# The scale of four RMS norms: a power of 256 columns on every partition in place of a power of two columns and a diagonal

## Chip, cores and metric

The kernel runs on one core of a Trainium2 chip. The metric is the device time of one execution in microseconds; the figure for the kernel before is the median of three runs. The traces come from one profiled execution. TensorE is called PE here (PEld is its weight load), VectorE DVE, ScalarE ACT, GpSimd POOL and SyncE SP; SP issues the transfers.

## What is computed

One step of a two-layer backbone for 128 context tokens and 128 latent tokens. Each layer has a mixer (layer 0: latent attention beside grouped-query attention; layer 1: differential attention) and a gated FFN with a width-3 convolution. Ahead of each mixer and each FFN, and once at the end, stands an RMS norm over the 2048 features of a token:

```python
def rmsnorm(x, g):
    xf = x.astype(jnp.float32)
    y = xf * lax.rsqrt(jnp.mean(xf * xf, axis=-1, keepdims=True) + EPS)
    return (y * g.astype(jnp.float32)).astype(x.dtype)
...
for l in range(DEPTH):
    mod = jax.nn.silu(cond) @ w_ada[l] + b_ada[l]
    sh1, sc1, gt1, sh2, sc2, gt2 = jnp.split(mod[:, None, :], 6, axis=-1)
    h = rmsnorm(x, g_norm_mix[l]) * (1 + sc1) + sh1
    m, new = mixer(h)
    x = x + gt1 * m
    h = rmsnorm(x, g_norm_ffn[l]) * (1 + sc2) + sh2
    x = x + gt2 * conv_ffn(h, ...)
return rmsnorm(x, g_final)
```

All weights are float32, and the adaLN product `silu(cond) @ w_ada` (two rows of condition against 2048 x 12288 per layer) is spread through the program, a piece at a time, beside the large products.

## The kernel before

**Layout.** Features lie on the 128 partitions and tokens on the free axis: `x` is a tile of 128 x 16 x 256, that is 16 chunks of 128 features, with the 128 context and 128 latent tokens side by side in 256 columns. The mean of squares of a token is therefore a sum over partitions, for which TensorE is used, and its scale is wanted on all partitions, since every chunk is multiplied by it column by column.

**Products.** Each float32 weight block is split into a high and a low half of type float32r (`split`: ACT makes `wh` by a cast, DVE makes `wl` by a subtraction), and the activations `hx` likewise. A block of 128x128 then takes three products of 256 columns (L299 to L301 for the first three output chunks after a norm, in `first_three`; L313, L314 and L317 elsewhere, in `gemm`).

**The norm's sums.** While the last product of a stage runs, `residual` adds each finished chunk to `x` (L569), ACT squares it into `sq` (L171), and POOL adds it to a running sum `sqacc` (L175). The square of the last chunk isn't added; it enters the sum as a second product.

**The scale before.** `stat_rstd` multiplies `sqacc` and `sq`, as the stationary operand, by a column of 1/2048: four products with one output column (L200, L201), which leave the mean of squares of each token on a partition, one column for the context tokens and one for the latent ones. `rstd` adds EPS on DVE (L183, 128x2) and takes the power -0.5 on POOL (L187, 128x2). `diagonal` multiplies the identity by each of the two columns (L207, two DVE instructions of 128x128), and `spread` multiplies `ones` by the result (L215, 128x256): the scale of each token stands on all partitions, in PSUM. This is done at four places after the opening: by `modulated` before the FFN of layer 0, before the mixer of layer 1 and before the FFN of layer 1, and by `norm_scale` at the end. The same helpers serve norms inside the mixers. The norm that opens layer 0 has sums of its own and is not touched.

**What follows the scale.** `modulate` makes `hx` chunk by chunk: DVE multiplies `x` by the scale (L510), DVE and ACT apply scale and shift (L516, L519), ACT casts to the high half (L520), and POOL or DVE subtracts for the low half (L505). `first_three` begins with the first chunks that are ready. At the end of the program, 16 DVE instructions (L1104) scale `x` into the result, and SP stores four chunks at a time.

**Order.** A scheduler with a timeline of its own orders the instructions of each engine; instructions under `keep_in_program_order` stay as written. In the two places of layer 1, `modulate` and `first_three` are so fixed; before the FFN of layer 0 they are not. `modulated` also carries a piece of the adaLN product: the tiles `araw` of `w_ada` (two buffers, four tiles of 1 MB a unit) are loaded by SP, `sum_rows` multiplies each (L427, four products of 512 columns), ACT copies the sum, and four PE transposes (L376) turn it. Some adaLN pieces run on DVE instead (`feature_sum`, L404).

Of the kernel before, what the change touches and what calls it, by code (L numbers as in the profile page):

```python
# [14 lines left out]
ALU = mybir.AluOpType  # L15
# [3 lines left out]
P = 128  # L19
D = 2048  # L20
KD = D // P
T = 128
NT = 2 * T
# [4 lines left out]
EPS = 1e-6  # L28
# [56 lines left out]
def step_kernel(ctx: ExitStack, tc: tile.TileContext, A: dict):  # L85
    nc = tc.nc
    pe, dve, act, pool, sp = nc.tensor, nc.vector, nc.scalar, nc.gpsimd, nc.sync
# [3 lines left out]
    tmp = ctx.enter_context(tc.tile_pool(name="tmp", bufs=2))  # L91
# [12 lines left out]
    def nm(s):  # L104
        uid[0] += 1
        return f"{s}_{uid[0]}"

    def T_(pl, shape, tag, dt=F32, bufs=None):
        kw = {} if bufs is None else {"bufs": bufs}
        return pl.tile(shape, dt, tag=tag, name=nm(tag), **kw)  # L110
# [8 lines left out]
    def C(name):  # L119
        a, w = _AT[name]  # L120
        return cst[:, a:a + w]

    ident, ones = C("ident"), C("ones")

    def inv(n):
        a = _AT["inv"][0] + INV[n]
        return cst[:, a:a + 1]
# [32 lines left out]
    def stat_init():  # L160
        return {"acc": None, "n": 0, "last": None}
# [15 lines left out]
    def rstd(cols, n, factor=1.0, out=None):  # L177

        v = T_(small, [P, 2], "rv")
        at = 0  # L180
        for ps in cols:
            w = n // len(cols)
            dve.tensor_scalar(out=v[:, at:at + w], in0=ps, scalar1=EPS, scalar2=factor ** -2,  # L183
                              op0=ALU.add, op1=ALU.mult)
            at += w
        r = T_(small, [P, 2], "rr") if out is None else out
        pool.tensor_tensor(out=r[:, :n], in0=v[:, :n], in1=C("mhalf")[:, :n], op=ALU.pow)  # L187
        return r

    def bank():  # L190
        return T_(pmisc, [P, 512], "misc")

    def att_bank():
        return T_(ppool["att"], [P, 512], "att", bufs=3)

    def stat_rstd(st, width, bank=bank, **kw):
        ps = bank()
        for g in range(2):
            t = slice(g * T, (g + 1) * T)
            pe.matmul(ps[:, g:g + 1], st["acc"][:, t], inv(width), start=True, stop=False)  # L200
            pe.matmul(ps[:, g:g + 1], st["last"][:, t], inv(width), start=False, stop=True)  # L201
        return rstd([ps[:, 0:2]], 2, **kw)

    def diagonal(r, cols):
        dg = T_(tmp, [P, 2 * T], "diag", bufs=1)
        for i, c in enumerate(cols):
            dve.tensor_scalar(out=dg[:, i * T:(i + 1) * T], in0=ident, scalar1=r[:, c:c + 1],  # L207
                              scalar2=None, op0=ALU.mult)
        return dg

    def spread(dg, cols=(0, 1), bank=bank):

        ps = bank()
        n = len(cols) * T
        pe.matmul(ps[:, :n], ones, dg[:, :n], start=True, stop=True)  # L215
        return ps[:, :n]
# [146 lines left out]
    def ada_finish(l, j, q):  # L363

        got = dict(ada)

        def copy():
            am = T_(tmp, [P, 512], "am", bufs=1)
            act.copy(am, got["ps"])
            got["am"] = am  # L370

        def turn(pin=None):
            pt = bank() if pin else T_(ppool["ada"], [P, 512], "ada", bufs=1)
            pin = pin or (lambda i: i)
            for b in range(4):
                pin(pe.transpose(pt[:, b * P:(b + 1) * P], got["am"][:, b * P:(b + 1) * P], ident))  # L376
            out = mod[:, l, j, 4 * q:4 * q + 4]
            dve.tensor_reduce(out=out, in_=pt.rearrange("p (b g r) -> p b r g", b=4, g=4)[:, :, 0:2],
                              axis=AX.X, op=ALU.add)
            biased(l, j, q)  # L380

        return [copy, turn]
# [40 lines left out]
    def sum_rows(t, raw, ps=None):  # L423
        if t == 0:
            ada["ps"] = ps or T_(ppool["ada"], [P, 512], "ada", bufs=1)
        for g in range(4):
            i = pe.matmul(ada["ps"][32 * g:32 * g + 32, :], condw[:, 4 * t + g, :], raw[:, g],  # L427
                          start=(t == 0), stop=(t == 3), skip_group_check=True)
            if pinned[0]:
                tc.keep_in_program_order(i)  # L430
# [53 lines left out]
    def ensure(l, j, qs=range(4)):  # L484
        for u in [(l, j, q) for q in qs]:
            while u in ROWS and ada["i"] <= ROWS.index(u):
                row_step()
            while u in FEATS and u not in done:
                feature_step()
            while u not in done:  # L490
                later.pop(0)()


    def norm_scale(st):
        return spread(diagonal(stat_rstd(st, D), (0, 1)))

    def modulate(hx, rb, l, which, chunks, fixed=False):


        pin = tc.keep_in_program_order if fixed else lambda i: i  # L500
        lows = []

        def low(c, h):
            eng = dve if (c % 4 == 0 if fixed else c % 2 == 0) else pool
            pin(eng.tensor_tensor(out=hx[:, c, NT:2 * NT], in0=h, in1=hx[:, c, :NT].bitcast(F32),  # L505
                                  op=ALU.subtract))

        for c in chunks:
            h = T_(tmp, [P, NT], "nt", bufs=4)
            pin(dve.tensor_tensor(out=h, in0=x[:, c], in1=rb, op=ALU.mult))  # L510
            for g in range(2):
                s = slice(g * T, (g + 1) * T)
                a_ = scl[:, l, which, c, g:g + 1]
                b_ = mod[:, l, 3 * which, c, g:g + 1]
                if g == 0:
                    pin(dve.tensor_scalar(out=h[:, s], in0=h[:, s], scalar1=a_, scalar2=b_,  # L516
                                          op0=ALU.mult, op1=ALU.add))
                else:
                    pin(act.activation(h[:, s], h[:, s], AF.Identity, scale=a_, bias=b_))  # L519
            pin(act.copy(hx[:, c, :NT], h))  # L520
            lows.append((c, h))
            if not fixed or len(lows) > 1:
                low(*lows.pop(0))
        for c, h in lows:
            low(c, h)

    def modulated(st, l, which, W, fixed):


        ensure(l, 3 * which + 1)  # L530
        ensure(l, 3 * which)
        while later:
            later.pop(0)()
        u = ROWS[ada["i"]]
        tile_ = lambda t: T_(wpool, [P, 4, 512], "araw", bufs=2)

        def load_tile(t):
            raw = tile_(t)
            sp.dma_start(out=raw, in_=A["w_ada"][u[0], u[1], u[2], t])
            return raw  # L540

        raws = [load_tile(0), load_tile(1)]
        hx = T_(keep, [P, KD, ROW], "hx", F32R)
        r = stat_rstd(st, D, att_bank)
        sum_rows(0, raws[0], bank())
        rb = spread(diagonal(r, (0, 1)), bank=att_bank)
        sum_rows(1, raws[1])
        raws += [load_tile(2), load_tile(3)]
        modulate(hx, rb, l, which, range(KD), fixed)
        ada["i"] += 1  # L550
        rest = ada_finish(*u)

        def last_rows():
            sum_rows(3, raws[3])
            rest[0]()

        def turn():
            rest[1](tc.keep_in_program_order)

        ps = first_three(W, lambda k: hx[:, k, :NT], lambda k: hx[:, k, NT:2 * NT],  # L560
                         AS_MADE if fixed else IN_TURN, lambda: sum_rows(2, raws[2]), fixed)
        if fixed:
            W.ahead(lambda i: i)
        return hx, ps, [last_rows, turn]
# [500 lines left out]
    with banks("pab") as ppool["ada"]:  # L1065
# [4 lines left out]
        ps = [bank(), att_bank()]  # L1070
# [9 lines left out]
        st = stat_init()  # L1080
# [4 lines left out]
    st = stat_init()  # L1085
    ffn(hx, W, ready, todo, 0, st)
    stage[0] = "c"
    with tc.tile_pool(name="cc", bufs=1) as cp, banks("pc") as ppool["ada"]:
        ada["pool"] = cp
        ppool["att"] = ppool["ada"]  # L1090
        W = Weights(A["w_in_c"], KD, 1)
        hx, ready, todo = modulated(st, 1, 0, W, True)
        load_cw(1)
        st = stat_init()
        ada["pew"] = PEW["c"]
        mixer_c(cp, hx, W, ready, todo, st)
        W = Weights(A["w_up"][1], KD, 1)
        hx, ready, todo = modulated(st, 1, 1, W, True)
    stage[0] = "ffn1"
    st = stat_init()  # L1100
    ffn(hx, W, ready, todo, 1, st)
    rb = norm_scale(st)
    for c in range(KD):
        dve.scalar_tensor_tensor(out=x[:, c], in0=x[:, c], scalar=C("gfin")[:, c:c + 1], in1=rb,  # L1104
                                 op0=ALU.mult, op1=ALU.mult)
# [132 lines left out]
```

## Time and profile before

| | us |
|---|---|
| median of 3 runs | 2371.13 (2369.91 to 2372.9) |
| profiled execution, its own time | 2370.48 |
| span of its trace (first to last instruction) | 2368.7 |
| TensorE busy | 2308.6 (97%) |
| DVE busy | 1798.8 (76%) |
| ACT busy | 1173.3 (50%) |
| POOL busy | 136.0 (6%) |

The mean granted clock of TensorE is 0.989 of full speed, and the DMA queues moved 610.81 MB. In a timeline each row gives the start, the time from the first start to the last end of the instructions merged in it, the engine, the line, the operation, the output and inputs by their names in the program, and in brackets how long the engine had been idle and what ended that. A row of the window table gives the busy time of each engine in a stretch of the span, with the count of its instructions, and at the end the granted clock, the share of DMA time and the rate. A row of a tile gives least, median and greatest duration in ns, and the first and last start.

### The profile page before, as it was taken

The page shows a single profiled execution, that of the slowest core. Times are in us where ns is not written, and L with a number is a line of the kernel's source. Part 1 is how long each engine was busy: PE and PEld are TensorE (multiplying, and loading weights), DVE is VectorE, ACT ScalarE, POOL GpSimd, SP SyncE. Part 2 cuts the span into 40 slices and gives each one's busy share as a digit, 9 for nine tenths or more (in the row PEclk, how much of TensorE's full clock was granted, in tenths as well). Part 3 has the DMA queues.
Part 4 walks back from the last instruction along what each step waited for, and adds up shares of the span by engine and source line. Part 5 has one row for each costly group of instructions (what it writes and reads, how often), then busy time and mean ns, then how long its engine had stood idle before and what let it go on. Part 6 is the DMA issues. An engine that isn't in the chain of part 4 may idle for free.

```text
span 2368.7 us, 47098 instructions
## 1 busy us (share of the span) xinstructions
PE 2308.6 (97%) x19626; PEld 2197.6 (93%) x19626; DVE 1798.8 (76%) x2677; ACT 1173.3 (50%) x1858; POOL 136.0 (6%) x133
## 2 busy tenths in 40 slices
PE   8899999999999999999999999998999999999997
PEld 6778878799999999999989999897999999999997
DVE  2667544579999999999968889799899755666654
ACT  4345553465554345554465555445555434555542
POOL 0001001100000000001220000022000000000011
PEclk9999999999999999999999999998999999999998
DMA  9886678867777876777767788776677555555553
GB/s 372 355 344 243 246 280 300 316 256 265 267 253 285 296 278 251 262 263 270 297 233 257 265 316 293 278 283 245 247 260 260 200 195 196 196 196 192 191 191 120
DMA packets 92421, 610.81 MB, mean 258 GB/s; under 512 B 9968, under 2 KB 17840, under 8 KB 20528
## 3 DMA queue, kind: packets, MB, share of 16 engines
q1 hardware_dynamic: 92208, 607.80, 69.6%
q8 instruction: 154, 2.52, 0.4%
q14 instruction: 59, 0.48, 0.1%
HBM read 603.01 MB, written 4.75 MB: 257 GB/s over the span
## 4 chain that ended last, share of the span: by engine, by line
PE 92%; DVE 3%; DMA 3%; issue 1%; ACT 1%; POOL 0%; POOLq 0%; DVEq 0%; ACTq 0%
PE acc L313 27%; PE acc L317 27%; PE acc L314 27%; PE ada L427 3%; DMA araw<-w_ada 2%; DVE wl L221 1%; PE acc L300 1%; PE acc L299 1%; DVE junk L404 1%; PE acc L301 1%; PE att L617 1%; PE misc L427 1%; PE att L940 0%; PE ada L340 0%; PE att L607 0%
## 5 line engine op out<-in xcount | busy, mean ns | idle before, releaser
L220 ACT CAST wh<-raw 128x1024 fp32r<-128x1024 f32 (+1 forms) x788 | 794.0, 1013 | 945.7 <-PE acc L314 770.8
L221 DVE TENSOR_TENSOR wl<-raw,wh 128x1024 fp32r<-128x1024 f32 (+1 forms) x788 | 922.4, 1185 | 343.3 <-ACT wh L220 324.3
L313 PE MATMUL acc<-hx,wh 128*128 128x256 f32 x4064 | 1131.1, 279 | 9.6 <-ACT wh L220 4.2
L317 PE MATMUL acc<-hx,wl 128*128 128x256 f32 x4064 | 1128.6, 278 | 1.0 <-DVE wl L221 1.0
L314 PE MATMUL acc<-hx,wh 128*128 128x256 f32 x4064 | 1129.2, 278 | 0.0
L313 PEld LDWEIGHTS acc<-hx,wh 128*128 128x128 f32 x4064 | 764.1, 188 | 35.5 <-issue 13.4
L317 PEld LDWEIGHTS acc<-hx,wl 128*128 128x128 f32 x4064 | 765.5, 188 | 9.2 <-issue 6.7
L314 PEld LDWEIGHTS acc<-hx,wh 128*128 128x128 f32 x4064 | 765.2, 188 | 6.5 <-issue 5.9
L404 DVE CUSTOM_DVE_ANT_0 junk<-araw,condb 128x2048 f32<-128x2048 f32 (+1 forms) x184 | 424.4, 2307 | 1.0 <-DMA araw<-w_ada 1.0
L314 PE MATMUL acc<-g,wh 128*128 128x256 f32 x1408 | 388.3, 276 | 0.0
L317 PE MATMUL acc<-g,wl 128*128 128x256 f32 x1408 | 388.0, 276 | 0.0
L313 PE MATMUL acc<-g,wh 128*128 128x256 f32 x1408 | 387.8, 276 | 0.0
L314 PEld LDWEIGHTS acc<-g,wh 128*128 128x128 f32 x1408 | 264.3, 188 | 0.0
L317 PEld LDWEIGHTS acc<-g,wl 128*128 128x128 f32 x1408 | 264.1, 188 | 0.0
L313 PEld LDWEIGHTS acc<-g,wh 128*128 128x128 f32 x1408 | 264.0, 188 | 0.0
L175 POOL TENSOR_TENSOR sqacc<-sqacc,sq 128x256 f32<-128x256 f32 x62 | 79.4, 1281 | 1582.0 <-issue 1286.7
L1017 ACT ACTIVATE cv<-acc,convw 128x256 f32<-128x256 f32 x176 | 98.3, 558 | 2.5 <-PE acc L301 2.5
L569 DVE SCALAR_TENSOR_TENSOR x<-acc,mod,x 128x128 f32<-128x128 f32 x192 | 57.9, 343 | 49.5 <-PE acc L317 49.5
L427 PE MATMUL ada<-araw,condw 128*32 128x512 f32 x608 | 82.3, 616 | 6.2 <-DMA araw<-w_ada 4.5
L1023 DVE SCALAR_TENSOR_TENSOR cv<-acc,convw,cv 128x254 f32<-128x254 f32 x176 | 84.3, 479 | 3.6
L1020 DVE SCALAR_TENSOR_TENSOR cv<-acc,convw,cv 128x254 f32<-128x254 f32 x176 | 83.5, 475 | 1.8 <-ACT cv L1017 1.8
L313 PE MATMUL acc<-oall,wh 128*128 128x256 f32 x208 | 58.2, 280 | 2.2 <-DVE x L569 2.2
(231 smaller groups left out, 1792.0 us busy)
## 6 DMA issues: line engine op xcount, KB each, us to landing
araw<-w_ada SPq DMA_DIRECT2D x186, 1024.0 KB, 5.4
raw<-w_up SPq DMA_DIRECT2D x176, 1024.0 KB, 4.8
raw<-w_down SPq DMA_DIRECT2D x88, 1024.0 KB, 4.8
raw<-w_in_c SPq DMA_DIRECT2D x48, 1024.0 KB, 5.2
raw<-w_in_ab SPq DMA_DIRECT2D x19, 1024.0 KB, 6.9
raw<-w_out_ab SPq DMA_DIRECT2D x16, 1024.0 KB, 7.0
raw<-w_out_c SPq DMA_DIRECT2D x16, 1024.0 KB, 5.0
raw<-w_ada SPq DMA_DIRECT2D x6, 1024.0 KB, 9.9
```

The lines of the kernel that those rows point to most:

```text
L175: pool.tensor_tensor(out=st["acc"], in0=st["acc"], in1=sq, op=ALU.add)
L220: pin(act.copy(out_hi, src))
L221: pin(dve.tensor_tensor(out=out_lo, in0=src, in1=out_hi.bitcast(F32), op=ALU.subtract))
L313: fixed(pe.matmul(ps[:, :n], wh, xh(k), start=(i == 0), stop=False))
L314: fixed(pe.matmul(ps[:, :n], wh, xl(k), start=False, stop=False))
L317: fixed(pe.matmul(ps[:, :n], wl, xh(k), start=False, stop=(i == last)))
L404: tc.keep_in_program_order(dve.tensor_tensor_reduce(out=junk, in0=raw, in1=condb[:, c].rearrange("p (g n) -> p g n", g=4), scale=1.0, scal ...
L427: i = pe.matmul(ada["ps"][32 * g:32 * g + 32, :], condw[:, 4 * t + g, :], raw[:, g], start=(t == 0), stop=(t == 3), skip_group_check=True)
L569: dve.scalar_tensor_tensor(out=x[:, c, s], in0=ps[:, s], scalar=mod[:, l, 3 * which + 2, c, g:g + 1], in1=x[:, c, s], op0=ALU.mult, op1=AL ...
L1017: pin(act.activation(y, ps, AF.Identity, scale=cw[:, 1, m:m + 1], bias=cw[:, 3, m:m + 1]))
L1020: pin(dve.scalar_tensor_tensor(out=y3[:, :, 1:], in0=p3[:, :, :T - 1], scalar=cw[:, 0, m:m + 1], in1=y3[:, :, 1:], op0=ALU.mult, op1=ALU.add))
L1023: pin(dve.scalar_tensor_tensor(out=y3[:, :, :T - 1], in0=p3[:, :, 1:], scalar=cw[:, 2, m:m + 1], in1=y3[:, :, :T - 1], op0=ALU.mult, op1=A ...
```

## The change

`norm_scale` makes the scale in another way, and `modulated` calls it. `ones` is the stationary operand, and `sqacc` and `sq` are multiplied by it with all their 256 columns (L497, L498): every partition of the result holds the sum of squares of each of the 256 tokens. One DVE instruction divides by 2048 and adds EPS (L500, 128x256, from PSUM into SBUF, in the buffer that the diagonal had), and one POOL instruction takes the power -0.5 of all 256 columns in place (L501, 128x256), with the exponent as one column broadcast. The scale is then read from SBUF and not from PSUM. In `modulated` the call stands ahead of the first row sum, where `stat_rstd` stood. Behind L504 all lines are 7 lower than before as far as `modulated` (L510 is now L517), and 6 lower behind it (L1104 is now L1110).

```diff
-    def norm_scale(st):
-        return spread(diagonal(stat_rstd(st, D), (0, 1)))
+    def norm_scale(st, bank=bank):
+
+        ps = bank()[:, :NT]
+        pe.matmul(ps, ones, st["acc"], start=True, stop=False)
+        pe.matmul(ps, ones, st["last"], start=False, stop=True)
+        rb = T_(tmp, [P, NT], "diag", bufs=1)
+        dve.tensor_scalar(out=rb, in0=ps, scalar1=1.0 / D, scalar2=EPS, op0=ALU.mult, op1=ALU.add)
+        pool.tensor_tensor(out=rb, in0=rb, in1=C("mhalf")[:, 0:1].to_broadcast([P, NT]), op=ALU.pow)
+        return rb
...
         raws = [load_tile(0), load_tile(1)]
         hx = T_(keep, [P, KD, ROW], "hx", F32R)
-        r = stat_rstd(st, D, att_bank)
+        rb = norm_scale(st, att_bank)
         sum_rows(0, raws[0], bank())
-        rb = spread(diagonal(r, (0, 1)), bank=att_bank)
         sum_rows(1, raws[1])
```

The order of TensorE before the FFN of layer 0, before the change (`att` is the PSUM tile of the norm, `ada` that of one adaLN unit, `acc` that of the first three output chunks):

```order
L317 MATMUL acc_4965<-hx_2390,wl_4954 128x256
L427 MATMUL ada_5020<-araw_4800,condw_79 32x512 x4
L427 MATMUL ada_5020<-araw_5018,condw_79 32x512 x4
L200 MATMUL att_5055<-cst_74,sqacc_3915 128x1
L201 MATMUL att_5055<-cst_74,sq_5016 128x1
L200 MATMUL att_5055<-cst_74,sqacc_3915 128x1
L201 MATMUL att_5055<-cst_74,sq_5016 128x1
L215 MATMUL att_5072<-diag_5069,cst_74 128x256
L427 MATMUL ada_5020<-araw_5025,condw_79 32x512 x4
L427 MATMUL ada_5020<-araw_5031,condw_79 32x512 x4
L299 MATMUL acc_5184<-hx_5054,wh_5187 128x256
```

The same place after the change (`misc` is the PSUM tile of the next adaLN unit):

```order
L317 MATMUL acc_4965<-hx_2390,wl_4954 128x256
L427 MATMUL ada_5020<-araw_4800,condw_79 32x512 x4
L427 MATMUL ada_5020<-araw_5018,condw_79 32x512 x4
L497 MATMUL att_5055<-sqacc_3915,cst_74 128x256
L498 MATMUL att_5055<-sq_5016,cst_74 128x256
L427 MATMUL ada_5020<-araw_5025,condw_79 32x512 x4
L427 MATMUL ada_5020<-araw_5031,condw_79 32x512 x4
L376 MATMUL ada_5043<-cst_74,am_5041 128x128 x4
L427 MATMUL misc_5061<-araw_5050,condw_79 32x512 x4
L427 MATMUL misc_5061<-araw_5052,condw_79 32x512 x4
L299 MATMUL acc_5176<-hx_5054,wh_5179 128x256
```

Besides the norm's own products, the turns of one adaLN unit (L376) and the first two row sums of the next have moved from among the products of `first_three` to ahead of the first of them.

The order of DVE before the mixer of layer 1, before the change (`rv`, `rr` and `diag` belong to the norm, `nt` is the chunk being modulated):

```order
L883 TENSOR_TENSOR lm_14313<-cst_74 128x2
L221 TENSOR_TENSOR wl_14146<-raw_14124,wh_14145 128x1024
L183 TENSOR_SCALAR rv_14006<-att_14001 128x2
L207 TENSOR_SCALAR diag_14015<-cst_74,rr_14008 128x128 x2
L510 TENSOR_TENSOR nt_14028<-x_76,att_14018 128x256
L516 TENSOR_SCALAR nt_14028<-nt_14028,scl_78,mod_77 128x128
```

and after it:

```order
L889 TENSOR_TENSOR lm_14297<-cst_74 128x2
L221 TENSOR_TENSOR wl_14130<-raw_14108,wh_14129 128x1024
L500 TENSOR_SCALAR diag_13996<-att_13993 128x256
L517 TENSOR_TENSOR nt_14012<-x_76,diag_13996 128x256
L523 TENSOR_SCALAR nt_14012<-nt_14012,scl_78,mod_77 128x128
L517 TENSOR_TENSOR nt_14017<-x_76,diag_13996 128x256
```

The diagonal steps are gone; the first chunk is multiplied by `diag`, which is now the scale that POOL writes, and nothing else stands between the vector step and that multiplication. On POOL the 128x256 power stands in each of the four places where the 128x2 power stood, and no other instruction of POOL has moved.

## The prediction

> **What bounds the kernel now.** I read the page first: shares, then the chain of work that ended last.
>
> ```profile
> span 2368.7 us, 47098 instructions
> PE 2308.6 (97%) x19626; PEld 2197.6 (93%) x19626; DVE 1798.8 (76%) x2677; ACT 1173.3 (50%) x1858; POOL 136.0 (6%) x133
> PE 92%; DVE 3%; DMA 3%; issue 1%; ACT 1%; POOL 0%; POOLq 0%; DVEq 0%; ACTq 0%
> ```
>
> TensorE is the bound nearly everywhere, and POOL is busy for 6%. That average says nothing about the four places that the change touches, so the busy time in their windows comes next. I call the norms N1 (after the first mixer), N2 (before the second), N3 (before the last FFN) and N4 (the end).
>
> ```profile
> core 0: us, PE busy (x) PEld busy (x) DVE busy (x) ACT busy (x) POOL busy (x), PEclk, DMA share, GB/s
> 1199.20:1202.30 3.10, 2.55 (x20) 1.29 (x24) 1.51 (x4) 0.00 (x0) 0.70 (x1) 1.00 0.92 226
> 1202.30:1226.00 23.70, 21.07 (x162) 17.76 (x162) 20.33 (x42) 18.53 (x40) 10.67 (x12) 1.00 0.67 266
> 1621.50:1627.00 5.50, 4.52 (x16) 2.06 (x16) 3.53 (x7) 0.01 (x1) 0.70 (x1) 0.50 0.70 225
> 2355.00:2358.80 3.80, 2.02 (x8) 1.24 (x8) 0.66 (x4) 0.03 (x1) 0.70 (x1) 0.71 0.00 0
> ```
>
> In each short window POOL runs one instruction of 0.70 us while ACT has nothing to do: everything waits for the scale. The main product is not running in it. So a longer POOL instruction there is paid in wall time, once per norm, unless something else holds that place. The timeline of N4 shows the chain itself:
>
> ```profile
> 2354.62 0.42 ACT L171 ACTIVATE sq<-x 128x256 f32<-128x256 f32 x1 [7.06 <-DVE x L569]
> 2355.55 0.36 PE L201 MATMUL misc<-cst,sq 128*128 128x1 f32 x2
> 2355.95 0.16 DVE L183 TENSOR_SCALAR rv<-misc 128x2 f32<-128x2 f32 x1 [1.43 <-PE misc L201]
> 2356.19 0.70 POOL L187 TENSOR_TENSOR rr<-rv,cst 128x2 f32<-128x2 f32 x1 [7.76 <-DVE rv L183]
> 2356.93 0.48 DVE L207 TENSOR_SCALAR diag<-cst,rr 128x128 f32<-128x128 f32 x2 [0.82 <-POOL rr L187]
> 2357.55 1.19 PE L215 MATMUL misc<-diag,cst 128*128 128x256 f32 x2 [1.64 <-DVE diag L207]
> 2358.79 6.35 DVE L1104 SCALAR_TENSOR_TENSOR x<-x,cst,misc 128x256 f32<-128x256 f32 x16 [1.38 <-PE misc L215]
> ```
>
> From the square's end (2355.04) to the first use of the scale (2358.79) are 3.75 us, one step after another.
>
> **The price that decides: the power on 256 columns, X.** The trace has powers of two columns only. The nearest rows on POOL, by tile and by group:
>
> ```profile
> L187 POOL TENSOR_TENSOR rsb<-rv,cst x8: 690/694/794, 223.8 to 300.6; 128x2 f32<-128x2 f32 x8
> L175 POOL TENSOR_TENSOR sqacc<-sqacc,sq x62: 731/1146/2224, 184.8 to 2347.7; 128x256 f32<-128x256 f32 x62
> L1219 POOL MEMSET const-float32-0.0<- 128x1 f32 x1 | 0.1, 99 | 0.2 <-issue 0.2
> ```
>
> Two columns of power take 0.69 us, as much as an undisturbed add takes for 256 (0.73). The smallest POOL instruction takes 0.10. What is left of the power is 0.59 us, or at most 295 ns a column; of the add (731 - 99) / 256 = 2.5 ns a column. Low end: the two columns are nearly all start, and the rest stream like the add's: 0.69 + 254 x 0.0025 = 1.33 us. High end: every column costs the same: 0.10 + 256 x 0.295 = 75.6 us. I take a value between, because a repeated calculation usually shares part of its start, but nearer the power's own row, which is the same operation on the same engine: two thirds of the way on a scale of ratios (the ends are a factor 118 apart), 2.5 x 118^(2/3) = 60 ns a column, **X = 0.69 + 254 x 0.060 = 15.9 us**. That is an estimate, and the weakest number here.
>
> The Trainium skill, GPSIMD Engine Reference, section 3.1, gives about 2.6 cycles an element for a two-input operation; at its 1.2 GHz that is 2.2 ns, and an estimate by it is X = 1.24 us. The add's row agrees with it (2.5 ns); no run here shows it for a power. By it the sum would be that of rival 2.
>
> **Part by part.** Removed per norm: four one-column products, the two-column vector step, the two-column power, two diagonal steps, the spreading product. Added: two products of 128x256 from `ones` (the first needs only the running sum, ready earlier), one vector step on 128x256 out of PSUM, X. The two records of one 128x256 fp32 product take 1.19 us in N4 and 0.70 at full clock in N2 (row below). The vector step on 256 columns I price at 0.42, by the L510 row with a PSUM operand. POOL starts some 0.1 after its producer and DVE 0.05 after POOL, as in N4.
>
> N4: 2355.04 + 1.19 + 0.42 + 0.15 + X = 2356.8 + X against 2358.79: **X - 1.9**. Nothing is behind it but the scaling and the stores.
>
> N2:
>
> ```profile
> 1198.74 0.41 ACT L171 ACTIVATE sq<-x 128x256 f32<-128x256 f32 x1
> 1201.58 0.70 PE L215 MATMUL att<-diag,cst 128*128 128x256 f32 x2 [0.55 <-DVE diag L207]
> 1202.32 0.42 DVE L510 TENSOR_TENSOR nt<-x,att 128x256 f32<-128x256 f32 x1 [0.79 <-PE att L215]
> 1205.40 0.38 PE L300 MATMUL acc<-hx,wh 128*128 128x256 f32 x1 [0.42 <-POOL hx L505]
> ```
>
> 1199.15 + 0.1 + 0.70 + 0.42 + 0.15 + X = 1200.5 + X against 1202.32: X - 1.8. Afterwards DVE is busy 20.33 of 23.70 us, so the modulation sets the pace and a late start is not made up. One loss more: this is the one norm where TensorE stays at full clock (1.00); after a wait of X it restarts at half, as in N1 and N3 now (N1's spacing of 0.21 below). Half clock for some 3.3 us loses 1.7 us of products; TensorE waits for hx in between anyway (0.42 in the last row), so between 0 and 1.7, I take 1.0: **X - 0.8**.
>
> The Trainium skill, TensorE: Matmul & The Clock Gate, Part 1, puts the fall of the clock at an idle time of about 3.4 us. By that a short X would spare N2 this 1.0 and a long one not; N2's full clock after a gap of 0.55 agrees.
>
> N3:
>
> ```profile
> 1622.06 2.28 DVE L404 CUSTOM_DVE_ANT_0 junk<-araw,condb 128x2048 bf16<-128x2048 f32 x1
> 1624.27 0.15 DVE L183 TENSOR_SCALAR rv<-att 128x2 f32<-128x2 f32 x1
> 1627.03 0.42 DVE L510 TENSOR_TENSOR nt<-x,att 128x256 f32<-128x256 f32 x1 [1.31 <-PE att L215]
> ```
>
> A feature sum holds DVE until 1624.27, and it still stands ahead of the new vector step, so the wider products hide behind it: 1624.27 + 0.42 + 0.15 + X = 1624.8 + X against 1627.03: **X - 2.2**.
>
> N1 is different, since the scale isn't alone there:
>
> ```profile
> 463.33 0.38 PE L200 MATMUL att<-cst,sqacc 128*128 128x1 f32 x2
> 467.19 1.41 DVE L510 TENSOR_TENSOR nt<-x,att 128x256 f32<-128x256 f32 x4 [1.31 <-PE att L215]
> 469.21 1.31 ACT L520 CAST hx<-nt 128x256 fp32r<-128x256 f32 x4
> 469.48 16.17 SPq L539 DMA_DIRECT2D araw<-w_ada  x4
> 469.96 1.93 PE L427 MATMUL ada<-araw,condw 128*32 128x512 f32 x8 [0.55 <-DMA araw<-w_ada]
> 471.83 1.01 PE L299 MATMUL acc<-hx,wh 128*128 128x256 f32 x3
> 472.63 0.41 PE L300 MATMUL acc<-hx,wh 128*128 128x256 f32 x1
> 472.85 0.41 PE L301 MATMUL acc<-hx,wl 128*128 128x256 f32 x1
> 477.00 0.60 PE L376 MATMUL ada<-cst,am 128*128 128x128 f32 x4
> 480.95 1.06 PE L427 MATMUL misc<-araw,condw 128*32 128x512 f32 x8
> 494.22 0.28 PE L313 MATMUL acc<-hx,wh 128*128 128x256 f32 x1
> 475.00:478.00 3.00, 3.00 (x24) 3.00 (x24) 1.11 (x4) 1.22 (x3) 1.01 (x2) 0.86 0.83 320
> 478.00:481.00 3.00, 3.00 (x31) 2.87 (x33) 3.00 (x11) 2.31 (x7) 0.75 (x1) 1.00 0.07 25
> ```
>
> hx exists from about 469.6 (2.4 after the scale's first use), yet its first product runs at 471.83: row sums behind a transfer hold it. The new order puts two more row sums and the four turns of L376 ahead of that product. Those sums read tiles issued from 469.48 on (the second once L427 at 469.96 has ended); the DMA share falls from 0.83 to 0.07 at 478, so they have landed by about 478.3. Two consequences. The products after the start shrink from 494.22 - 471.83 = 22.4 to 22.4 - 2 x 1.06 - 0.60 = 19.7 us. And they can't start before 478.3 + 1.06 = 479.4, even if the scale is early: a loss of 479.4 + 19.7 - 494.2 = 4.9 us at the least. With the two wide products at half clock for most of their time (0.70 to 1.22 each, 2.0 in all), the scale is there at 463.33 + 2.0 + 0.42 + 0.15 + X = 465.9 + X, and the end is at 465.9 + X + 2.4 + 19.7 = 488.0 + X: **X - 6.2**, and this decides above X = 11.1.
>
> **Sum.** 4X - 6.2 - 0.8 - 2.2 - 1.9 = 4X - 11.1 = +52.5 us for X = 15.9. The profiled execution took 2370.5 us beside its span of 2368.7; it lies 0.6 under the runs' median of 2371.1, which is inside their spread. 2370.5 + 52.5 = **2423 us**. No cover is counted for the four X: the other POOL work of these places (the low halves, L505) comes after the scale, and ACT and DVE wait for it too.
>
> **Rivals.** (1) *Every column pays in full.* X = 75.6: 4 x 75.6 - 11.1 = +291, 2662 us. For it: the same operation, and 0.69 us for two columns is hard to read as start alone beside a start of 0.10. Against: part of the 0.59 may be paid once.
> (2) *The power streams like the add.* X = 1.33: N2, N3, N4 give 1.33 - 1.8, 1.33 - 2.2 and 1.33 - 1.9, together -1.9; N1 costs 4.9 through the row sums, in all +3.0, 2373 us; if their tiles land before the scale, N1 costs nothing and it is 2369. Either way not measurably slower. It decides for X under about 2 us. For it: only the add's row; against: the two-column power's 0.69.
> (3) *Only the moved row sums tell*, with X between 2 and 5: 4.9 + 3X - 4.9, plus 6 to 15 us, 2377 to 2385. In N1 the TensorE queue waits for a transfer and not for POOL.
>
> **How the numbers follow.** Forecast (X from 5 to 40): 0.56, its own range 2385 to 2519. Rival 1: 0.28. Rival 2: 0.10. Rival 3: 0.03. Faster by something I don't see, such as a better place of the weight splits in the new order: 0.03. A change under 0.2% (4.7 us) can't be told from none here. Slower: 0.56 + 0.28 + 0.03 and 0.01 of rival 2 = 0.88; same 0.09; faster 0.03. The range runs from 2378 (X near 3.5) to 2665, to take in rival 1's time; left out are rival 2, the faster cases and full columns that cost more than 75.6.
>
> **What would show it.** POOL's rows at L501: four of 128x256, by their duration X itself. DVE's first L517 and L1110 must wait for POOL in all four places; today they wait for PE. The window of N2 must show a clock under 1.00. In N1 the first L299 must stand after two more L427 groups, behind POOL if X is over 11, behind a transfer if not. It's wrong if L501 takes under 3 us, or if the span grows by much less than four times L501's duration less 11.

## The result and the profile after

The changed kernel takes 2558.46 us (median of 5 runs: 2526.35, 2531.86, 2558.46, 2558.87, 2582.22) against 2371.13. The ratio is 1.072, 95% interval 1.067 to 1.077: slower, by 187 us at the median where 52 were forecast. Here and below, a run over 1.5% above the fastest of its kernel counts as slow and is left out of the ratio. The runs lie in steps of about 27 us, which is treated below. The profiled execution is the slowest of the five, 2582.22 us with a span of 2580.4, and was 211.7 us longer than the profiled execution of before (2580.4 - 2368.7).

First the page of the kernel after: span, engines, and the chain that ended last.

```profile
span 2580.4 us, 47044 instructions
PE 2369.5 (92%) x19602; PEld 2254.2 (87%) x19602; DVE 1804.8 (70%) x2669; ACT 1167.8 (45%) x1858; POOL 296.9 (12%) x133
PE 85%; POOL 5%; DVE 5%; issue 2%; POOLq 2%; ACT 1%; DMA 1%; DVEq 0%; ACTq 0%
```

POOL's busy time has grown by 160.9 us (296.9 - 136.0), TensorE's share has fallen from 97% to 92%, and POOL, 0% of the chain before, is now 5% of it. TensorE's busy time has also grown, by 60.9 us, though it runs 24 instructions fewer; that is a second effect. The first is in the tile of the scale (the row of its power) and in the waits of the whole span (total, times, longest):

```profile
L501 POOL TENSOR_TENSOR diag<-diag,cst x4: 41126/41132/41136, 464.2 to 2529.3; 128x256 f32<-128x256 f32 x4
```

```profile
DVE nt L517 <- POOL diag L501: 114.3, 3, 41.2
DVE x L1110 <- POOL diag L501: 41.2, 1, 41.2
```

X is 41.13 us in all four places, with a spread of 10 ns. DVE stands still behind it four times. At N4 the timeline shows the same chain as before with other links:

```profile
2527.59 0.42 ACT L171 ACTIVATE sq<-x 128x256 f32<-128x256 f32 x1 [7.36 <-DVE x L575]
2528.05 0.70 PE L498 MATMUL misc<-sq,cst 128*128 128x256 f32 x2 [0.78 <-ACT sq L171]
2528.79 0.42 DVE L500 TENSOR_SCALAR diag<-misc 128x256 f32<-128x256 f32 x1 [1.30 <-PE misc L498]
2529.30 41.13 POOL L501 TENSOR_TENSOR diag<-diag,cst 128x256 f32<-128x256 f32 x1 [8.19 <-DVE diag L500]
2570.46 1.67 DVE L1110 SCALAR_TENSOR_TENSOR x<-x,cst,diag 128x256 f32<-128x256 f32 x4 [41.24 <-POOL diag L501]
```

Product, vector step and power follow each other at once, and POOL runs for 41.13 us with nothing beside it. The windows of the four norms show what is idle meanwhile (busy time of PE, PEld, DVE, ACT and POOL, then granted clock, DMA share, GB/s):

```profile
464.00:505.00 41.00, 7.98 (x36) 1.47 (x36) 0.44 (x3) 0.58 (x1) 40.84 (x1) 0.55 0.44 172
1269.00:1310.00 41.00, 3.19 (x11) 2.68 (x12) 4.62 (x11) 3.46 (x9) 37.92 (x4) 0.51 0.11 47
1731.00:1772.00 41.00, 1.94 (x8) 0.20 (x8) 0.23 (x1) 0.00 (x0) 40.74 (x1) 0.54 0.22 87
2530.00:2570.00 40.00, 0.00 (x0) 0.00 (x0) 0.00 (x0) 0.00 (x0) 40.00 (x1) 0.54 0.00 0
```

At N1 the row sums fill 8 us of TensorE, and in the other windows little or nothing runs beside POOL. The granted clock is near half in each, in N2 too, where it was 1.00. At N1 the power, the row sums and what follows them read as below (the last row is the end of the FFN behind N1):

```profile
464.16 41.14 POOL L501 TENSOR_TENSOR diag<-diag,cst 128x256 f32<-128x256 f32 x1 [6.07 <-DVE diag L500]
474.21 1.94 PE L427 MATMUL misc<-araw,condw 128*32 128x512 f32 x8 [1.25 <-DMA araw<-w_ada]
478.56 1.93 PE L427 MATMUL misc<-araw,condw 128*32 128x512 f32 x8 [2.41 <-DMA araw<-w_ada]
505.33 1.43 DVE L517 TENSOR_TENSOR nt<-x,diag 128x256 f32<-128x256 f32 x4 [31.94 <-POOL diag L501]
507.78 1.01 PE L299 MATMUL acc<-hx,wh 128*128 128x256 f32 x3 [27.29 <-ACT hx L527]
530.48 0.36 PE L313 MATMUL acc<-hx,wh 128*128 128x256 f32 x1 [1.74 <-DVE cv L1029]
1261.07 0.28 PE L317 MATMUL acc<-g,wl 128*128 128x256 f32 x1
```

The moved row sums end at 480.5, while the first L299 waits until 507.78: it stands behind POOL's scale, not behind a transfer.

**The four norms, measured.** I take each norm from the start of the last large product ahead of it to the start of the first large product (L313) behind the first three chunks, and N4 from the last product to the end. N1 was 494.22 - 461.27 = 32.95 us and is 530.48 - 460.43 = 70.05. In the same way:

| | before | after | longer by | forecast's formula with X = 41.13 |
|---|---|---|---|---|
| N1 | 32.95 | 70.05 | 37.1 | X - 6.2 = 34.9 |
| N2 | 28.70 | 69.63 | 40.9 | X - 0.8 = 40.3 |
| N3 | 34.79 | 73.80 | 39.0 | X - 2.2 = 38.9 |
| N4 | 15.10 | 53.87 | 38.8 | X - 1.9 = 39.2 |
| sum | | | 155.8 | 4X - 11.1 = 153.4 |

**The rest: a second pace of the products.** Of 211.7 us some 54 lie in the two FFNs, in which nothing was changed. From the first L313 of the FFN of layer 0 to its last L317 it was 1197.53 - 494.22 = 703.31 us and is 1261.07 - 530.48 = 730.59; in layer 1 703.43 and 730.48. One window of TensorE in the middle of each FFN, before and then after (busy time, count of the products that touch the window, granted clock, DMA share, GB/s):

```profile
800.00:840.00 40.00, 40.00 (x356) 1.00 0.81 304
1900.00:1940.00 40.00, 40.00 (x355) 1.00 0.55 197
```

```profile
800.00:840.00 40.00, 40.00 (x342) 1.00 0.76 282
1900.00:1940.00 40.00, 40.00 (x342) 1.00 0.69 249
```

TensorE is busy throughout at full granted clock in both, with 356 products in such a window in one and 342 in the other: a product starts every 113.3 ns before and every 117.8 ns after, by the start times of the trace. The single intervals in these windows are 113 or 114 ns before and 116 to 119 ns after, so it isn't a matter of a few waits; and the transfers give no sign of setting it, since the slower pace has the lower DMA share at 800. Over an FFN of some 6,200 products 4.5 ns make 27 to 28 us. The steps of 27 us between the runs of after fit none, one or two FFNs at the slower pace; the profiled one has two. The norms (155.8 us) and the FFNs (54.3) leave 1.6 of the 211.7 us.

### The profile page after: what moved, and what is told of

It is laid out like the page before. It is cut to its first block, busy times and chain, and to the rows that moved or that the text cites. A ratio compares the mean times of both kernels' runs of the same rounds, so it can differ in the third digit from the quotient of the medians.

```text
span 2580.4 us, 47044 instructions
## 1 busy us (share of the span) xinstructions
PE 2369.5 (92%) x19602; PEld 2254.2 (87%) x19602; DVE 1804.8 (70%) x2669; ACT 1167.8 (45%) x1858; POOL 296.9 (12%) x133
## 4 chain that ended last, share of the span: by engine, by line
PE 85%; POOL 5%; DVE 5%; issue 2%; POOLq 2%; ACT 1%; DMA 1%; DVEq 0%; ACTq 0%
PE acc L313 26%; PE acc L314 26%; PE acc L317 26%; POOL diag L501 5%; PE ada L427 3%; POOLq L1231 2%; DVE wl L221 1%; DVE nt L517 1%; DVE junk L404 1%; DVE nt L523 1%; PE att L623 1%; DMA araw<-w_ada 0%; PE att L946 0%; ACT wh L220 0%; PE att L613 0%
## 5 line engine op out<-in xcount | busy, mean ns | idle before, releaser
L313 PE MATMUL acc<-hx,wh 128*128 128x256 f32 x4064 | 1145.8, 283 | 11.4 <-ACT wh L220 4.2
L317 PE MATMUL acc<-hx,wl 128*128 128x256 f32 x4064 | 1141.7, 281 | 0.9 <-DVE wl L221 0.9
L314 PE MATMUL acc<-hx,wh 128*128 128x256 f32 x4064 | 1142.4, 281 | 0.0
L313 PEld LDWEIGHTS acc<-hx,wh 128*128 128x128 f32 x4064 | 776.8, 191 | 38.1 <-issue 13.4
L317 PEld LDWEIGHTS acc<-hx,wl 128*128 128x128 f32 x4064 | 765.3, 188 | 9.2 <-issue 6.7
L314 PEld LDWEIGHTS acc<-hx,wh 128*128 128x128 f32 x4064 | 765.4, 188 | 6.4 <-issue 5.9
L314 PE MATMUL acc<-g,wh 128*128 128x256 f32 x1408 | 395.5, 281 | 0.0
L317 PE MATMUL acc<-g,wl 128*128 128x256 f32 x1408 | 395.3, 281 | 0.0
L313 PE MATMUL acc<-g,wh 128*128 128x256 f32 x1408 | 395.1, 281 | 0.0
L313 PEld LDWEIGHTS acc<-g,wh 128*128 128x128 f32 x1408 | 270.0, 192 | 0.0
L314 PEld LDWEIGHTS acc<-g,wh 128*128 128x128 f32 x1408 | 264.5, 188 | 0.0
L317 PEld LDWEIGHTS acc<-g,wl 128*128 128x128 f32 x1408 | 264.3, 188 | 0.0
L501 POOL TENSOR_TENSOR diag<-diag,cst 128x256 f32<-128x256 f32 x4 | 164.5, 41131 | 29.9 <-DVE diag L500 22.4
L299 PE MATMUL acc<-hx,wh 128*128 128x256 f32 x144 | 42.6, 306 | 105.4 <-ACT hx L527 104.4
L299 PEld LDWEIGHTS acc<-hx,wh 128*128 128x128 f32 x144 | 29.3, 209 | 112.7 <-ACT hx L527 109.6
L517 DVE TENSOR_TENSOR nt<-x,diag 128x256 f32<-128x256 f32 x48 | 24.4, 518 | 114.4 <-POOL diag L501 114.3
```

The lines of the kernel that those rows point to most:

```text
L299: pin(pe.matmul(ps[c][:, :NT], wh, xh(k), start=a, stop=False))
L313: fixed(pe.matmul(ps[:, :n], wh, xh(k), start=(i == 0), stop=False))
L314: fixed(pe.matmul(ps[:, :n], wh, xl(k), start=False, stop=False))
L317: fixed(pe.matmul(ps[:, :n], wl, xh(k), start=False, stop=(i == last)))
L501: pool.tensor_tensor(out=rb, in0=rb, in1=C("mhalf")[:, 0:1].to_broadcast([P, NT]), op=ALU.pow)
```

## Experiments

Two theories stood at first. **Duration:** the loss is X four times less 11.1 us, and X is the power's own price by the column. **Restart:** the pace of the FFNs is drawn by the long idle time of TensorE ahead of them. The kernel before ran beside all of them.

**no_power: the new form with a cheap instruction in the power's place.** The power is left out, so the scale is not the norm's.

```diff
-        pool.tensor_tensor(out=rb, in0=rb, in1=C("mhalf")[:, 0:1].to_broadcast([P, NT]), op=ALU.pow)
+        pool.tensor_tensor(out=rb, in0=rb, in1=inv(D).to_broadcast([P, NT]), op=ALU.mult)
```

> The wide form with a POOL multiply of 128x256 in place of the power (the power is left out; everything else of the change stays). Theory: all of the loss hangs on the power's 41.1 us; with X = 0.75 the other terms stand alone, N2 -1.1, N3 -1.5, N4 -1.2, and N1 near 0 since its two moved row sums are mostly not moved here: about 2367, between 2365 and 2371, and products at a pace of 113 ns throughout. Rival (the wide products, the scale in SBUF or the new order cost something of their own): over 2376, or a pace of 118 ns in an FFN.

Measured: 2373.35 us (2368.18 to 2375.62, 10 runs) against 2371.42, ratio 1.0007 (0.9998 to 1.0016): no change that can be told. The multiply took 612 ns in all four places, the products of both FFNs kept 113.3 ns, and none of the ten runs stood a step higher. So the power's duration carries the loss, and the form itself gains nothing even when its slow step is cheap. The median came out 2 us above the range I expected, and the trace says where: N2 +0.6 and N4 -1.7 us lie within 0.8 of the formula (-0.2 and -1.3 at X = 0.61), N1 at -0.4, but N3 at +2.9 where X - 2.2 = -1.6 was expected. The timeline of N3 in this kernel, then rows of N3 before:

```profile
1624.58 0.42 ACT L171 ACTIVATE sq<-x 128x256 f32<-128x256 f32 x1 [3.19 <-DVE x L575]
1628.89 0.43 DVE L517 TENSOR_TENSOR nt<-x,diag 128x256 f32<-128x256 f32 x1 [0.65 <-POOL diag L501]
1633.01 1.93 PE L427 MATMUL misc<-araw,condw 128*32 128x512 f32 x8 [4.87 <-DMA araw<-w_ada]
1634.87 0.58 PE L299 MATMUL acc<-hx,wh 128*128 128x256 f32 x1
```

```profile
1621.10 0.42 ACT L171 ACTIVATE sq<-x 128x256 f32<-128x256 f32 x1 [3.21 <-DVE x L569]
1629.82 1.93 PE L427 MATMUL misc<-araw,condw 128*32 128x512 f32 x8 [2.83 <-DMA araw<-w_ada]
1631.69 0.58 PE L299 MATMUL acc<-hx,wh 128*128 128x256 f32 x1
```

In both, the first L299 starts right behind a row sum that waited for its transfer. Counted from the start of the last square, the first use of the scale came 1.6 us sooner, as the formula has it (4.31 us against 1627.03 - 1621.10 = 5.93), but the first L299 only 0.3 us sooner (10.29 us against 10.59). So at N3 an early scale was worth next to nothing, since a transfer held the same place. The other 3.2 us lie outside the scale's path: the last square came 1.4 us later behind the last large product, and from the first L299 to the first L313 it took 1.8 us longer, 1.30 of it a wait of TensorE for a weight split on DVE. (In this kernel the scheduler had put the moved row sums and turns of N1 back behind the first products, so the floor of 4.9 us that the prediction saw there was not tried.)

**widths: the price of the power by itself.** The kernel before with powers of several widths on POOL behind its last work.

```diff
+    for n in (1, 2, 4, 8, 16, 32, 64, 128):
+        fix(pool.tensor_tensor(out=o[:, :n], in0=a[:, :n], in1=C("mhalf")[:, 0:1].to_broadcast([P, n]), op=ALU.pow))
+    fix(pool.tensor_tensor(out=o, in0=a, in1=e, op=ALU.pow))
+    fix(pool.tensor_tensor(out=o[0:16], in0=a[0:16], in1=e[0:16], op=ALU.pow))
+    fix(pool.tensor_tensor(out=o, in0=C("ones")[:, 0:1].to_broadcast([P, NT]), in1=e, op=ALU.pow))
+    for n in (2, 256):
+        fix(pool.tensor_tensor(out=o[:, :n], in0=a[:, :n], in1=C("mhalf")[:, 0:1].to_broadcast([P, n]), op=ALU.mult))
```

> The kernel before with 13 more POOL instructions at its end, on scratch. Theory (0.37 + 0.159 us a column): powers of 1, 2, 4, 8, 16, 32, 64 and 128 columns take 0.53, 0.69, 1.0, 1.6, 2.9, 5.5, 10.5 and 20.7 us; 256 columns with a full tile of exponents and another output tile 41.1, the same on 16 partitions, the same with a base of ones; multiplies of 2 and 256 columns 0.1 to 0.2 and 0.73. Rival 1 (broadcast or in place is what costs): the full tile of exponents far under 41. Rival 2 (columns pay in steps, or from some width on): a bend in the first eight.

The groups of POOL at the end of that kernel, each one instruction (busy us, mean ns; L1117 to L1120 are powers, L1122 multiplies):

```profile
L1118 POOL TENSOR_TENSOR nt<-nt,nt 128x256 f32<-128x256 f32 x1 | 41.2, 41226 | 0.1
L1119 POOL TENSOR_TENSOR nt<-nt,nt 16x256 f32<-16x256 f32 x1 | 41.2, 41216 | 0.1
L1120 POOL TENSOR_TENSOR nt<-cst,nt 128x256 f32<-128x256 f32 x1 | 41.1, 41115 | 0.1
L1117 POOL TENSOR_TENSOR nt<-nt,cst 128x128 f32<-128x128 f32 x1 | 20.7, 20726 | 0.1
L1117 POOL TENSOR_TENSOR nt<-nt,cst 128x16 f32<-128x16 f32 x1 | 2.9, 2893 | 0.1
L1117 POOL TENSOR_TENSOR nt<-nt,cst 128x2 f32<-128x2 f32 x1 | 0.7, 704 | 0.1
L1117 POOL TENSOR_TENSOR nt<-nt,cst 128x1 f32<-128x1 f32 x1 | 0.6, 555 | 0.0
L1122 POOL TENSOR_TENSOR nt<-nt,cst 128x256 f32<-128x256 f32 x1 | 0.6, 612 | 0.1
L1122 POOL TENSOR_TENSOR nt<-nt,cst 128x2 f32<-128x2 f32 x1 | 0.2, 194 | 0.1
```

From 16 to 128 columns the price rises by (20726 - 2893) / 112 = 159 ns a column, and less the columns at that price 0.32 to 0.40 us are left at every width up to 128 and about as much at 256: **a start of some 0.38 us and 0.16 us a column**. Sixteen partitions cost as much as 128, and a full tile of exponents, another output tile or a base of ones change it by 0.3% at most from the 41.13 of the changed kernel. A multiply on 256 columns costs (612 - 194) / 254 = 1.6 ns a column, a hundred times less.

**half_power: X halved.** The power on 128 of the 256 columns, the multiply on the others, from which the power is left out.

```diff
-        pool.tensor_tensor(out=rb, in0=rb, in1=C("mhalf")[:, 0:1].to_broadcast([P, NT]), op=ALU.pow)
+        pool.tensor_tensor(out=rb[:, :T], in0=rb[:, :T], in1=C("mhalf")[:, 0:1].to_broadcast([P, T]), op=ALU.pow)
+        pool.tensor_tensor(out=rb[:, T:], in0=rb[:, T:], in1=inv(D).to_broadcast([P, T]), op=ALU.mult)
```

> The power on the 128 context columns only; the latent columns get a POOL multiply instead (their power is left out). Theory (a start of 0.37 and 0.159 us a column): X = 20.7 + 0.4, 4 x 21.1 - 11.1 = +73, 2444, and 27 or 54 more in runs in which products keep a slower pace. Rival (the price is one of the instruction, its broadcast exponent or its writing in place, and not of its columns): X over 35, 2500 or more.

Measured: 2447.96, 2448.65, 2450.93 and 2474.28 us, ratio 1.036 (1.031 to 1.040). POOL's two groups:

```profile
L501 POOL TENSOR_TENSOR diag<-diag,cst 128x128 f32<-128x128 f32 x4 | 82.9, 20732 | 29.6 <-DVE diag L500 22.1 <-DVE mod L386 7.6
L502 POOL TENSOR_TENSOR diag<-diag,cst 128x128 f32<-128x128 f32 x4 | 1.6, 400 | 0.0
```

With X = 20.73 + 0.40 the formula gives 2371.4 + 4 x 21.13 - 11.1 = 2444.8; the lower three runs lie 3 to 6 us above it, and the fourth, the profiled one, a step higher, with its first FFN at 730.59 us and its second at 703. The loss goes with the power's duration.

**last_only: one place of the four.** `modulated` keeps the old scale; only the last norm is wide.

```diff
         raws = [load_tile(0), load_tile(1)]
         hx = T_(keep, [P, KD, ROW], "hx", F32R)
-        rb = norm_scale(st, att_bank)
+        r = stat_rstd(st, D, att_bank)
         sum_rows(0, raws[0], bank())
+        rb = spread(diagonal(r, (0, 1)), bank=att_bank)
         sum_rows(1, raws[1])
```

> Only the norm at the end has the wide power; the three others are as before. Theory: X - 1.9 with X = 41.1, so +39.2, 2410, with the runs within 2 us of each other because no large product follows the wait. Rival (the slower pace of products comes with the program, not with a wait ahead of them): about 2437 or 2465 in some runs, and a pace of 118 ns in an FFN.

Measured: 2406.82, 2408.28, 2409.45 and 2409.93 us, ratio 1.0159 (1.0142 to 1.0176), L501 once at 41.14 us. That is about +38 against X - 1.9 = 39.2. None of these runs stood a step higher, though they lie 3 us apart and not 2. The fifth execution, the profiled one, took 2948.51 us at a mean granted clock of 0.746, so only the duration of L501 is taken from it; the pace of its FFNs can't be read.

**hold_long and hold_short: the wait without the wide form.** The kernel before, with 55 or 12 multiplies on POOL ahead of the narrow power in the four norms.

```diff
-        r = stat_rstd(st, D, att_bank)
+        r = stat_rstd(st, D, att_bank, hold=HOLD)
...
+        if hold:
+            w = T_(tmp, [P, NT], "nt", bufs=4)
+            pool.memset(w, 1.0)
+            pool.tensor_copy(out=w[:, :n], in_=v[:, :n])
+            for _ in range(hold):
+                pool.tensor_tensor(out=w, in0=w, in1=C("ones")[:, 0:1].to_broadcast([P, NT]), op=ALU.mult)
+            v = w
```

> The kernel before (narrow power, diagonal) with 55 POOL multiplies by one of 128x256, at 0.69 us from start to start, ahead of the narrow power in the four norms: a wait of some 38 us without the wide power, the wide products or a scale in SBUF. Theory (a long wait ahead of a stage is what lets its products keep the slower pace of 118 ns): about 2371 + 4 x 38 less some 4 us of slack, 2515 to 2525, in some runs 27 or 54 more, each 27 with an FFN at 118 ns in the trace. Rival (the pace comes with the wide form): all runs within 5 us of each other, every FFN at 113 ns.

> The same with 12 multiplies, a wait of some 8.5 us. Theory: about 2371 + 4 x 8.5 less some 5 of slack, 2395 to 2405; if any restart from half clock can draw the slower pace, some runs 27 above; if it takes tens of us of waiting, none. Rival (the pace comes with the wide form): none either, so this run speaks only beside the long one.

Measured, long: 2522.50, 2525.95, 2549.50, 2550.96, 2553.44, 2555.72 us, ratio 1.071 (1.065 to 1.077). Short: 2403.78, 2427.61, 2430.04, 2433.86, 2457.97, 2459.29, ratio 1.022 (1.016 to 1.027). The lowest runs are where the waits alone put them, and above them stand one step or two. So neither the power nor the wide form is needed for the slower pace; a wait that lengthened the gaps ahead of the two FFNs by 5.5 and 6.0 us is enough (N1 38.43 against 32.95, N3 40.82 against 34.79). In the same session one of eleven runs of the kernel before stood at 2398.22, the others at 2368 to 2374: by its time, it can draw that pace too, though seldom.

**busy_pe: the changed kernel with TensorE kept at work.** 96 products of `ones` with `x` into a bank that nobody reads, behind the row sums of N1, N2 and N3.

```diff
+        busy = T_(pacc, [P, 512], "acc")
+        for i in range(BUSY):
+            tc.keep_in_program_order(pe.matmul(busy[:, :NT], ones, x[:, i % KD], start=True, stop=True))
```

> The change itself, with 96 products of ones and x (128x256, read by nobody) on TensorE during the wait in the first three norms, some 41 us at full clock. Theory (an idle TensorE draws the slower pace): clock near 1.00 through the waits, every FFN at 113 ns, all runs within 6 us of each other at 2515 to 2530. Rival (the pace follows from the break in the main products or from the wide form, busy or not): some runs still 27 or 54 above the lowest.

Measured: 2540.43, 2544.16, 2545.58, 2568.08, 2569.80, 2595.90 us, ratio 1.076 (1.071 to 1.082). The expectation failed twice. The lowest runs are higher than those of the changed kernel, since at N1 the products (L557 here) began only behind the last row sum and outlasted the power (N1 took 82.0 us against 70.05):

```profile
466.76 41.14 POOL L502 TENSOR_TENSOR diag<-diag,cst 128x256 f32<-128x256 f32 x1 [6.07 <-DVE diag L501]
482.78 43.86 PE L557 MATMUL acc<-x,cst 128*128 128x256 f32 x192
```

And the steps of 27 us are still there. At N1 the FFN's products followed these at once, and at N3 too, so TensorE had been at work for more than 40 us ahead of either FFN; by the times the slower pace is drawn all the same, in both FFNs in the run of 2595.90. (The profiled run is one of the lowest, with both FFNs at 113.3 ns.) The restart theory in this form falls.

**hold_ffn0 and hold_mixer: where the wait stands.** The long hold at one norm only.

```diff
-        r = stat_rstd(st, D, att_bank, hold=HOLD)
+        r = stat_rstd(st, D, att_bank, hold=HOLD if (l, which) == (0, 1) else 0)
```

(In hold_mixer `(1, 0)`; the last norm has no hold in either.)

> The kernel before, with 55 multiplies on POOL ahead of its narrow power (a wait of some 38 us) at N1 alone, right before the FFN of layer 0. The wait itself costs 37.5 us (N1's gap was 70.42 against 32.95 in the long hold at all four places), so the lowest runs are to stand near 2408. Theory A (the slower pace is drawn by the FFN that follows a wait for the scale): some runs stand 27 us above the lowest, none 54, and where the profiled run is one of these its products of the first FFN are 117.8 ns apart and those of the second 113.3. Theory B (the pace is drawn by a stage anywhere, whatever precedes it, about as often as in the kernel before, one run in 24): nearly all five runs within 5 us of the lowest.

> The same wait at N2 alone, before the mixer of layer 1; both FFNs keep what stands ahead of them in the kernel before. The wait costs 38.9 us (N2's gap was 67.55 against 28.70 in the long hold), lowest runs near 2409. Theory A (the FFN right behind a wait draws the pace): no run 27 us above the lowest. Theory C (a wait anywhere earlier draws it in a later FFN): some runs 27 us above, the second FFN at 117.8 ns in a profile of such a run. Theory B (whatever precedes): nearly all within 5 us.

Measured, ahead of the FFN of layer 0: 2408.61, 2412.34, 2415.18, 2436.19, 2437.09, 2438.80 us. Ahead of the mixer: 2404.21, 2404.76, 2406.64, 2408.05, 2410.24. Windows of the profiled runs, the former (a run a step higher) first:

```profile
800.00:840.00 40.00, 40.00 (x342) 1.00 0.76 280
1900.00:1940.00 40.00, 40.00 (x356) 1.00 0.61 211
```

```profile
800.00:840.00 40.00, 40.00 (x356) 1.00 0.75 276
1900.00:1940.00 40.00, 40.00 (x355) 1.00 0.53 186
```

With the wait ahead of the first FFN, three of six runs stand a step higher and none two; in the profiled one the FFN behind the wait is the slower, and the other keeps its pace. With the wait ahead of the mixer no run of five does. For the FFNs that is as theory A had it. Over all these kernels, by the steps between the runs, 23 of the 60 FFNs with an added wait at the norm ahead of them ran at the slower pace, and 1 of 118 in the runs of the kernel before, no_power, last_only and hold_mixer.

But the wait right ahead isn't the whole of it. The kernel before has both paces in its own profile: the same products in the mixer of layer 1 start every 117.8 ns from 1326 to 1345 and every 113.3 ns from 1366 to 1385.

```profile
1326.00:1345.00 19.00, 19.00 (x164) 1.00 0.93 338
1366.00:1385.00 19.00, 19.00 (x170) 1.00 0.81 288
```

The output product of that mixer, a stage of some 73 us, shows both as well: it ran fast before, and at the slower pace in hold_mixer and also in widths, where no wait is added ahead of it. So the wait in hold_mixer, some 300 us earlier, can't be taken for its cause (the rows are of before, hold_mixer and widths):

```profile
1560.00:1600.00 40.00, 40.00 (x356) 1.00 0.80 289
```

```profile
1600.00:1640.00 40.00, 40.00 (x342) 1.00 0.79 287
```

```profile
1560.00:1600.00 40.00, 40.00 (x342) 1.00 0.79 293
```

Nor does a slow FFN start slow. In the profile after, the first FFN's products behind N1 start at the faster pace, 18 of them in 2.04 us (first two rows), until four adaLN turns break their stream at 540.18; behind these, 18 take 2.12 us (last two rows), and so on to the end of the FFN:

```profile
536.32 0.28 PE L314 MATMUL acc<-hx,wh 128*128 128x256 f32 x1
538.36 0.28 PE L314 MATMUL acc<-hx,wh 128*128 128x256 f32 x1
540.18 0.60 PE L376 MATMUL misc<-cst,am 128*128 128x128 f32 x4
541.09 0.28 PE L313 MATMUL acc<-hx,wh 128*128 128x256 f32 x1
543.21 0.28 PE L313 MATMUL acc<-hx,wh 128*128 128x256 f32 x1
```

In all twenty FFNs of the ten profiles other than last_only's, the last break is at these turns, some 10 us behind the first L313, and the 6,100 products behind it keep one pace; all five slow ones ran at 113.3 ns right ahead of the turns. Nor does any longer stream in these profiles change its pace without a break. So the pace is settled where the stream of products is broken and taken up again, and held until the next break. How a wait ahead of the FFN raises the chance of the slower one stays open: it isn't the idle time of TensorE (busy_pe), nor does it take a long wait (hold_short), nor the granted clock within the FFN, which is 1.00 at either pace.

## Why the prediction was wrong

The direction, the mechanism of the waits and all four signs to look for held; the time of 2423 us did not, though the range to 2665 holds it. Of the 135 us between forecast and median, 4 x (41.13 - 15.9) = 101 are X; most of the rest is a step of 27 us, one FFN at the slower pace.

1. **The step that failed is the price X**: 15.9 us as put, 41.13 as measured, a factor of 2.6. It was read from one width, two columns at 0.69 us, which can't tell a start from a price by the column. Measured, the start is 0.38 (not the 0.10 of the smallest POOL instruction), so the two columns were 0.31 us of work and 0.16 us each. My low end priced all of the 0.69 as start, and I chose 60 ns between 2.5 and 295 by a ratio rule that no row supported. The forecast's own span, X from 5 to 40, ended just below the measured value. Had I taken as start a POOL instruction of the same kind with two inputs (here 0.19 us for a multiply of 2 columns, a row that before doesn't have), (0.69 - 0.19) / 2 = 0.25 us a column would have made 64 us: too high, but the right order.
2. **The sum around X held.** With X = 41.13 the formula gives 2370.5 + 153.4 = 2524 us; the two lowest runs were 2526 and 2532. N2, N3 and N4 came within 0.6 us. (At N3 that is partly chance: the scale came 38.9 us later behind the last square, as X - 2.2 has it, while that square came 1.1 us sooner behind the last large product and the stretch behind the scale took 1.2 us longer.) N1 came 2.2 over: the scale began 0.9 us earlier than I had it, but the first three chunks took 22.70 us (530.48 - 507.78) and not 19.7. Taking the row sums out from among them freed no time, since TensorE then waited in that place, 1.74 us of it for the convolution on DVE (the L313 row at N1). Two slips in the arithmetic carry no weight: 2356.8 + X against 2358.79 is X - 2.0, not X - 1.9, and the lower end of the range, 2378, goes with an X near 2.5 by the working for X under 11, not near 3.5.
3. **No cover for X**: right, as the windows show. That N1 is decided by POOL above X = 11: right (L299 at 507.78). That N2 loses its full clock: right (0.51 in its window).
4. **The term put at nothing is the pace of the two FFNs**, 0, 27 or 54 us of a run and 54 of the profiled one. The forecast took the large products outside the four norms as unchanged. The profile before held the second pace, in layer 1's mixer, but I read only the windows of the norms. hold_ffn0 shows that a wait right ahead of an FFN raises the chance of it (three of six runs); by what, stays open.
5. **The rivals.** Every column in full (X = 75.6) had the right reading, that the power is paid by the column, with too small a start. The power that streams like the add was ruled out by widths, and the estimate of 1.24 us that stands beside it in the prediction falls with it; no_power shows that its price, 2369 to 2373 us, would have been right had POOL's step been that cheap, but by chance: N1, where it saw a loss of 4.9 us, lost nothing, and N3 lost 2.9. That only the moved row sums tell was ruled out by X and by the wait of the first L299 at N1.

No version came out ahead of both: with the power replaced by an instruction of 0.61 us the wide form only equals the kernel before, so what is left to gain in this form is about nothing.

## What to carry to other kernels

A duration known at one width gives no price by the column: where an instruction is widened a hundredfold, the start has to come from a second width or from an instruction of the same kind, and a wide interval is all that one row allows. Where an expensive elementwise function is wanted on all partitions, do it on the narrowest form and spread the result: here the diagonal and its product cost 1.9 us of N4's path (2356.93 to 2358.79) and the wide power 41. A wait of some microseconds ahead of a long TensorE stage may cost more than itself, so compare the start-to-start time of the products behind it, in the profile before too, and not their busy share alone.

## What the hardware showed that I had not expected

The power on POOL costs 0.38 us and 0.16 us a column on 16 partitions as on 128 (41.22 us for 16x256, 41.23 for 128x256), where a multiply of 128x256 takes 0.61. And products of one shape, at a granted clock of 1.00 and with TensorE busy throughout, have two paces, 113.3 and 117.8 ns from start to start, each held from one break of their stream to the next, here for an FFN of 703 or 730 us. By its time, the kernel before drew the slower one in an FFN in one run of 40 here.
